# Four additions of a gate/up pair in one adding DMA, and a fourth seven-product block in the seven pairs that have it

## The chip, the cores and the metric

The kernel runs on one core of one Trainium2 chip. The metric is the device time of one execution in microseconds (us), the median of several runs.

## The reference

One decoder layer in float32 for 256 tokens, model width 2048. Two mixers (a retention branch and a sliding-window attention with sinks) work on one input projection of 2048 to 12,800 columns, are merged by two sigmoid gates, go through an output projection, and a first layer norm follows. Then comes the part that this change touches most, the feed-forward sublayer with inner width 5632, and a second layer norm:

```python
h = layer_norm(DEEPNORM_ALPHA * h + merged @ w_out[l], ln1_g[l], ln1_b[l])
ffn = (jax.nn.silu(h @ w_gate[l]) * (h @ w_up[l])) @ w_down[l]
h = layer_norm(DEEPNORM_ALPHA * h + ffn, ln2_g[l], ln2_b[l])
```

## The kernel before, in words

**Products.** Every float32 operand is split into a rounded high part and the remainder (ACT casts `wh`, DVE subtracts to get `wl`), and one product is three matmuls: high by high, high by low, low by high (L324 to L326). A matmul has 128 rows and 512 columns.

**Pairs.** Large weight matrices are worked on in pairs of 512-column blocks. For a gate/up pair `f` (class `PairChunk`, L247) the two columns are the gate's and the up's; the two rows are the two halves of the tokens. The depth of 2048 is cut into eight k pairs, each one weight load of 1 MB. An ordinary k pair ("s") is 2 x 2 x 2 = 8 products; a seven-product one ("S") computes the same from 7 products of sums (the Winograd form, L248): its step "R" has three products and its step "T" four. For S, DVE forms sums of the weights (`tsum`, L290 to L292), ACT and DVE split them (`th`, `tl`), and only three of the four original blocks are split. The sums of the left operand are made once (`hsums`, L966). The order of the k pairs is `pair_seq(n)` (L771): S and s in turn for the n seven-product ones, then the rest ordinary. `NQ` is n for gate/up pairs and `NS` for the three parts of the down projection.

A pair accumulates in eight PSUM banks, which is all of them: P1, P5, P6, P7 hold shared products, and C11, C12, C21, C22 what belongs to one result. After the last T step `mids` (L728) copies P1 (ACT) and adds the others to four tiles s1, vx, w, x5 (DVE). After the last step `done_gu` (L994) adds C11 to C22 to them and computes silu(gate) x up. Then four transposes for each half of the tokens bring it into the form that the down projection wants (`u_bg`, L922), and `psums` (L962) makes its sums.

**Parts.** The eleven pairs of the inner width (f = 0 is done by ordinary chunks) are done in parts 0 to 3, 4 to 7, 8 to 10. After each part the down projection adds its share to the residual: two down pairs after the first two parts, one and two ordinary chunks after the last.

**Order.** `Stream` (L339) issues loads, splits and matmuls step by step: loads run `LOOK_B` = 3 blocks ahead, splits as far as there are slots (three for `wh`/`wl`, one for `th`/`tl`). After each step background jobs advance by `PC` = 2 half-steps. The framework then orders each engine's queue by these priorities and adds the waits, unless an instruction is pinned in program order. Weight loads are issued on SP's queue; ACT's queue has two small loads at the start; POOL issues none.

**Start.** The first chunk loads x and its weights together in blocks of `XS` k tiles (L440). While the first one is on its way, PE runs warm-up matmuls (L434 to L438).

Of the kernel before, what the change touches and what calls it, by code (L numbers as in the profile page):

```python
# [14 lines left out]
RIGHT = "right"  # L15
# [12 lines left out]
NWARM = 3  # L28
TD = 14
CP = 1  # L30
NQ = 3
NX = 2
PG = 4
NGEN = 3
# [65 lines left out]
def layer_kernel(ctx, tc, a, out):  # L100
# [233 lines left out]
                self.done(self)  # L334

    LOOK_B = 3
    XB = 4

    class Stream:  # L339
        def __init__(self):  # L340
# [13 lines left out]
        def ahead(self):  # L354
            while True:
                cb = self.casts[min(self.ci, len(self.casts) - 1)][2]
                while self.bi < min(len(self.blocks), cb + LOOK_B):
                    ch, b = self.blocks[self.bi]
                    ch.dma(b)
                    self.bi += 1  # L360
                if self.ci >= len(self.casts):
                    return
                ch, i, _ = self.casts[self.ci]
                nm, cap = ch.slot(i)
                if self.live.get(nm, 0) >= cap:
                    return
                if self.ci in self.precast:
                    self.precast.pop(self.ci)()
                ch.cast(i)
                self.ci += 1  # L370
                self.live[nm] = self.live.get(nm, 0) + 1
# [16 lines left out]
    jobs = {}  # L388

    NC0 = P + NFR  # L390
    cst = const.tile([P, LINE * -(-NC0 // LINE)], F32, name="cst")
    ident = cst[:, 0:P]
    freq = cst[:, P:NC0]
    halfpi = const.tile([P, LINE], F32, name="halfpi")[:, 0:1]
    nc.gpsimd.memset(halfpi, math.pi / 2)

# [22 lines left out]
    dmask = msk[:, 0:RH * 384].rearrange("p (h c) -> p h c", h=RH)  # L419
    bmask = msk[:, RH * 384:]  # L420
    sinks = xa.tile([P, LINE], F32, name="sinks")[:, 0:NH]
    cosr = xa.tile([P, 2, NFL], F32, name="cosr")[:, :, 0:NFR]
    sinr = xa.tile([P, 2, NFL], F32, name="sinr")[:, :, 0:NFR]
    sinn = xa.tile([P, 2, NFL], F32, name="sinn")[:, :, 0:NFR]
# [9 lines left out]
    for i in range(NWARM):  # L434
        wp = bank("tr", [P, C])
        nc.tensor.matmul(wp, lhsT=warm[:, 0:P], rhs=warm[:, P:P + C], start=True, stop=True)
    wp = bank("tr", [P, C])
    nc.tensor.matmul(wp[:, 0:SEQ], lhsT=warm[:, 0:P], rhs=warm[:, P:P + SEQ], start=True, stop=True)  # L438

    XS = [1, 1, 2, 2, 2, 2, 2, 2, 2]  # L440
    xraw = {}

    def x_dma(b):
        k = sum(XS[:b])
        r = ini.tile([P, max(XS), SEQ + C], F32, name="xraw", bufs=XB)
        nc.sync.dma_start(out=r[:, 0:XS[b]], in_=a["xw"][:, k:k + XS[b]])
        xraw[b] = r
        if b == 2:
            nc.scalar.dma_start(out=cst[:, 0:NC0], in_=a["consts"][:, 0:NC0])
            xraw["pos"] = xa.tile([P, LINE], I32, name="posi")[:, 0:2]  # L450
            nc.scalar.dma_start(out=xraw["pos"], in_=a["pos"])

# [115 lines left out]
    def attention(g, t, q):  # L568
# [10 lines left out]
        W = nk * P  # L579
        per = C // W  # L580
        sm = ap_.tile([P, 8, W], F32, name="sm")
        mx = small.tile([P, 8], F32, name="mx8")
        sums = small.tile([P, 8], F32, name="sums")
        mk = bmask[:, P:2 * P] if t == 0 else bmask
        for j in range(4 // per):
            sps = [bank("mx", [P, per, W]) for _ in range(2)]
# [4 lines left out]
            for h, u, i in hs:  # L591
                nc.vector.tensor_tensor_reduce(out=sm[:, h], in0=sps[u][:, i], in1=mk, scale=HD ** -0.5,
                                               scalar=sinks[:, g * 8 + h:g * 8 + h + 1],
                                               op0=ALU.add, op1=ALU.max, accum_out=mx[:, h:h + 1])
        es = small.tile([P, 8], F32, name="es")
        nc.vector.tensor_sub(out=es, in0=sinks[:, g * 8:g * 8 + 8], in1=mx)
        nm = small.tile([P, 8], F32, name="nm")
        nc.vector.tensor_scalar(out=nm, in0=mx, scalar1=-1.0, scalar2=None, op0=ALU.mult)
        nc.scalar.activation(out=es, in_=es, func=AF.Exp)
        for h in range(8):  # L600
# [126 lines left out]

    def mids(ch):  # L728
        tp, acc = sc["tp"], ch.acc
        s1 = tp.tile([P, C], F32, name="s1")  # L730
        vx = tp.tile([P, C], F32, name="vx")
        w = tp.tile([P, C], F32, name="w")
        x5 = tp.tile([P, C], F32, name="x5")
        nc.scalar.copy(out=s1, in_=acc["P1"])
        nc.vector.tensor_add(out=vx, in0=s1, in1=acc["P6"])
        nc.vector.tensor_add(out=w, in0=vx, in1=acc["P5"])
        nc.vector.tensor_add(out=vx, in0=vx, in1=acc["P7"])
        nc.vector.tensor_add(out=x5, in0=vx, in1=acc["P5"])
        ev["t"] = (s1, vx, w, x5)

    def done_va(ch, j):
        acc = ch.acc
# [158 lines left out]
    sgf = {}  # L901
    ujobs = []
    parts = ((0, 4), (4, 8), (8, 11))
    NS = (3, 3, 2)
    f0_of = {f: f0 for f0, f1 in parts for f in range(f0, f1)}
    ND = {f: n for (f0, f1), n in zip(parts, NS) for f in range(f0, f1)}

    def done_g(ch, t, c):
        if t == 0:
            sgf[c] = sc["fp"].tile([P, 2, C], F32, name="sg2", bufs=1)  # L910
        nc.scalar.activation(out=sgf[c][:, t], in_=ch.acc[t], func=AF.Silu)

    def done_u(ch, t, c):
# [45 lines left out]
    def lhs_s(kp, i):  # L959
        return sc["sh"][:, i, kp], sc["sl"][:, i, kp]  # L960

    def psums(ph, pl, k0, n):  # L962
        yield
        yield from hsums(ph, pl, sc["psh"], sc["psl"], n, k0)

    def hsums(hh, hl, sh, sl_, n, k0=0):  # L966
        for kp in range(n):
            h2 = sc["tp"].tile([P, 2, 2, P], F32, name="s1")
            sm = sc["tp"].tile([P, 4, P], F32, name="vx")
            ks = slice(2 * kp, 2 * kp + 2)  # L970
            nc.vector.tensor_add(out=h2.rearrange("p k t c -> p k (t c)"), in0=hh[:, ks].bitcast(F32), in1=hl[:, ks].bitcast(F32))
            nc.vector.tensor_add(out=sm[:, 0], in0=h2[:, 0, 1], in1=h2[:, 1, 1])
            nc.vector.tensor_sub(out=sm[:, 1], in0=sm[:, 0], in1=h2[:, 0, 0])
            nc.vector.tensor_sub(out=sm[:, 2], in0=h2[:, 0, 1], in1=h2[:, 0, 0])
            nc.vector.tensor_sub(out=sm[:, 3], in0=h2[:, 1, 0], in1=sm[:, 1])
            split_evict(sh[:, :, k0 + kp], sl_[:, :, k0 + kp], sm)
            yield
# [4 lines left out]

    def flush():
        if "u" in ev:
            f, args = ev.pop("u")
            queue_p(f, [Job(u_bg(*arg)) for arg in args])

    def queue_p(f, js):
        kp = 2 * (f - f0_of[f])
        n = min(2, ND[f] - kp)  # L990
        if n > 0:
            jobs["ps", f] = Job(psums(*pTs[f], kp, n), js)

    def done_gu(ch, f):  # L994
        acc = ch.acc
        s1, vx, w, x5 = ev["t"]
        sg = sc["fp"].tile([P, 2, C], F32, name="sg2", bufs=1)
        pTs[f] = (sc["pp"].tile([P, 4, SEQ], F32R, name="ph"), sc["pp"].tile([P, 4, SEQ], F32R, name="pl"))
        nc.vector.tensor_add(out=sg[:, 0], in0=s1, in1=acc["C11"])
        nc.scalar.activation(out=sg[:, 0], in_=sg[:, 0], func=AF.Silu)  # L1000
        nc.vector.tensor_add(out=w, in0=w, in1=acc["C12"])
        nc.vector.tensor_add(out=sg[:, 1], in0=vx, in1=acc["C21"])
        nc.scalar.activation(out=sg[:, 1], in_=sg[:, 1], func=AF.Silu)
        nc.vector.tensor_mul(out=sg[:, 0], in0=sg[:, 0], in1=w)
        nc.vector.tensor_add(out=x5, in0=x5, in1=acc["C22"])
        nc.vector.tensor_mul(out=sg[:, 1], in0=sg[:, 1], in1=x5)
        ev["u"] = f, [(sg, t, *pTs[f]) for t in range(2)]
        if f + 1 in (4, 8, 11):
            flush()

    seq = pair_seq(NQ)
    for part, (f0, f1) in enumerate(parts):
        for f in range(f0, f1):
            if f == 0:
                stream.add(Chunk([a["w_gu0"][0, b] for b in range(KT // KB)], KT, lhs_h, lambda ch, t: done_g(ch, t, 0),
                                 order=stagger_first(4), wide=True))
                mark_d = len(stream.steps)
                stream.add(Chunk([a["w_gu0"][1, b] for b in range(KT // KB)], KT, lhs_h, lambda ch, t: done_u(ch, t, 0)))
                mark_u = len(stream.steps)
            else:  # L1020
                stream.add(PairChunk([a["w_gu"][f - 1, kp] for kp in range(KT // 2)], seq, lhs_h, lhs_s, mid_gu,
                                     lambda ch, f=f: done_gu(ch, f)))
        if part == 2:
            mark_e = len(stream.steps)
# [63 lines left out]
    sc["hres"] = hp.tile([P, 2, DM], F32, name="hres")  # L1088
    sc["hh"] = hp.tile([P, KT, SEQ], F32R, name="hh")
    sc["hl"] = hp.tile([P, KT, SEQ], F32R, name="hl")  # L1090
    sc["sh"] = hp.tile([P, 4, NQ, P], F32R, name="sh")
    sc["sl"] = hp.tile([P, 4, NQ, P], F32R, name="sl")
    sc["stats"] = hp.tile([P, 2, 4, 8], F32, name="stats1")[:, :, :, 0:6]
    nc.sync.dma_start(out=sc["hres"], in_=a["x"].rearrange("(t p) d -> p t d", p=P))
    gains = {}
    for nm in ("ln1_g", "ln1_b"):
# [7 lines left out]
    sc["pp"] = ppc.enter_context(tc.tile_pool(name="pp", bufs=4, side=RIGHT))  # L1104
    sc["tp"] = ppc.enter_context(tc.tile_pool(name="tp", bufs=1, side=RIGHT))
    sc["sp2"] = ppc.enter_context(tc.tile_pool(name="sp2", bufs=1, side=RIGHT))
    pq = ppc.enter_context(tc.tile_pool(name="pq", bufs=1, side=RIGHT))
    sc["psh"] = pq.tile([P, 4, max(NS), P], F32R, name="psh")
    sc["psl"] = pq.tile([P, 4, max(NS), P], F32R, name="psl")
    Job(hsums(sc["hh"], sc["hl"], sc["sh"], sc["sl"], NQ))  # L1110
    stream.run(mark_u, PC)
    banks(("all", 8))
    sc["stats"] = hp.tile([P, 2, 4, 8], F32, name="stats2")[:, :, :, 0:6]
    stream.run(mark_e, PC)
    for nm, tg in (("ln2_g", "hh"), ("ln2_b", "hl")):
        gains[nm] = hp.tile([P, DM], F32, name=tg)
        nc.sync.dma_start(out=gains[nm], in_=bcast_cols(a[nm], 0, DM))
    sc["zg"] = hp.tile([P, C], F32, name="sh")
    sc["dg"] = hp.tile([P, 2, P], F32, name="sl")
    stream.run(len(stream.steps), PC)  # L1120
    drain()

# [79 lines left out]
```

## Time and profile before

| | |
|---|---|
| median of 3 runs | 1432.5 us (1432.46 to 1432.58) |
| the profiled execution | 1432.52 us, its span 1430.7 us |
| granted TensorE clock, mean | 0.999 |
| weight loads of gate/up | 88 of 1 MB, median 4.9 us to landing |

The rows of the trace stand in a section of their own below. "Waits" give which engine and line waited for what, the sum in us, how often, and the longest. The chain is the work that ended last, followed back. A window's row gives its start and end, its length, the busy time (and number of instructions) of PE, PEld, DVE, ACT and POOL in it, the granted clock, the DMA engines' busy share and GB/s.

### The profile page before, as it was taken

What the parts mean: (1) busy time and instruction counts of PE and PEld (TensorE: products, weight loads), DVE (VectorE), ACT (ScalarE), POOL (GpSimd) and SP (SyncE); (2) the same over time, 40 slices, a digit from 0 to 9 for tenths busy, and PEclk for the clock granted to TensorE, in tenths of its full rate; (3) what the DMA queues carried; (4) which work ended last, traced back from release to release, by engine and by line L of the source; (5) the groups of instructions that cost most, each with busy time, mean ns of one, the idle gap of its engine ahead of it and who ended that gap; (6) DMA issues with size and microseconds to landing.
All of it is one profiled execution on the core that took longest, in us unless ns stands there. A gap on an engine that the chain in (4) does not pass through costs nothing.

```text
span 1430.7 us, 16141 instructions
## 1 busy us (share of the span) xinstructions
PE 1423.1 (99%) x6494; PEld 1165.0 (81%) x6494; DVE 1135.0 (79%) x1271; ACT 699.3 (49%) x664; POOL 0.9 (0%) x6
## 2 busy tenths in 40 slices
PE   9999999999999999999999999999999999999998
PEld 6878888878888878788888888888888888888886
DVE  6764555487878879776589989888999988898986
ACT  5465444344445445444345555445555455455542
POOL 0000000000000000000000000000000000000000
PEclk9999999999999999999999999999999999999999
DMA  8643433446554655567454555555555555555662
GB/s 327 222 158 118 143 115 122 150 174 210 198 209 166 210 188 206 206 244 272 160 177 177 208 184 211 193 209 193 196 195 206 206 206 181 197 211 200 213 234 88
DMA packets 40235, 274.75 MB, mean 192 GB/s; under 512 B 4704, under 2 KB 4832, under 8 KB 8160
## 3 DMA queue, kind: packets, MB, share of 16 engines
q1 hardware_dynamic: 39440, 272.79, 53.4%
q8 instruction: 51, 0.84, 0.2%
q10 hardware_dynamic: 720, 0.92, 0.2%
q14 instruction: 24, 0.20, 0.0%
HBM read 271.60 MB, written 2.10 MB: 191 GB/s over the span
## 4 chain that ended last, share of the span: by engine, by line
PE 98%; DVE 1%; DMA 0%; ACT 0%; SPq 0%; issue 0%
PE bank L324 21%; PE bank L326 21%; PE bank L325 21%; PE acc L235 9%; PE acc L233 9%; PE acc L234 9%; PE tr L540 2%; PE mx L589 2%; PE mx L618 1%; PE bank L540 1%; PE bank L235 1%; PE bank L234 1%; PE bank L233 1%; DMA xraw<-in_xw 0%; PE bank L685 0%; PE mx L656 0%
## 5 line engine op out<-in xcount | busy, mean ns | idle before, releaser
L304 ACT CAST wh<-raw 128x2048 fp32r<-128x2048 f32 (+1 forms) x174 | 307.7, 1769 | 295.1 <-PE bank L326 223.8
L305 DVE TENSOR_TENSOR wl<-raw,wh 128x2048 fp32r<-128x2048 f32 (+1 forms) x174 | 366.4, 2108 | 62.0 <-ACT wh L304 61.6
L218 DVE TENSOR_TENSOR wl<-raw,wh 128x2048 fp32r<-128x2048 f32 x70 | 160.1, 2288 | 79.6 <-ACT wh L217 79.3
L217 ACT CAST wh<-raw 128x2048 fp32r<-128x2048 f32 x70 | 133.5, 1909 | 175.0 <-PE acc L235 110.8
L324 PE MATMUL bank<-wh,hh 128*128 128x512 f32 x460 | 179.6, 390 | 0.0
L326 PE MATMUL bank<-wh,hl 128*128 128x512 f32 x460 | 179.1, 389 | 0.0
L325 PE MATMUL bank<-wl,hh 128*128 128x512 f32 x460 | 179.0, 389 | 0.0
L305 DVE TENSOR_TENSOR tl<-tsum,th 128x2048 fp32r<-128x2048 f32 x58 | 132.6, 2287 | 34.2 <-ACT th L304 34.0
L304 ACT CAST th<-tsum 128x2048 fp32r<-128x2048 f32 x58 | 111.0, 1914 | 95.1 <-DVE tsum L292 78.0
L324 PE MATMUL bank<-wh,xh 128*128 128x512 f32 x364 | 144.5, 397 | 0.0
L326 PE MATMUL bank<-wh,xl 128*128 128x512 f32 x364 | 141.8, 389 | 0.0
L325 PE MATMUL bank<-wl,xh 128*128 128x512 f32 x364 | 141.7, 389 | 0.0
L233 PE MATMUL acc<-wh,xh 128*128 128x512 f32 x352 | 140.9, 401 | 0.4 <-ACT wh L217 0.3
L235 PE MATMUL acc<-wh,xl 128*128 128x512 f32 x352 | 138.7, 394 | 0.0
L234 PE MATMUL acc<-wl,xh 128*128 128x512 f32 x352 | 138.0, 392 | 0.7 <-DVE wl L218 0.7
L326 PEld LDWEIGHTS bank<-wh,hl 128*128 128x128 f32 x460 | 86.3, 188 | 18.0
L325 PEld LDWEIGHTS bank<-wl,hh 128*128 128x128 f32 x460 | 86.4, 188 | 17.8
L324 PEld LDWEIGHTS bank<-wh,hh 128*128 128x128 f32 x460 | 86.4, 188 | 17.7
L324 PE MATMUL bank<-wh,ph 128*128 128x512 f32 x220 | 85.9, 390 | 0.0
L325 PE MATMUL bank<-wl,ph 128*128 128x512 f32 x220 | 85.6, 389 | 0.0
L326 PE MATMUL bank<-wh,pl 128*128 128x512 f32 x220 | 85.1, 389 | 0.0
L324 PEld LDWEIGHTS bank<-wh,xh 128*128 128x128 f32 x364 | 68.3, 188 | 15.8 <-issue 1.4
(287 smaller groups left out, 2315.2 us busy)
## 6 DMA issues: line engine op xcount, KB each, us to landing
raw<-in_w_gu SPq DMA_DIRECT2D x88, 1024.0 KB, 4.9
raw<-in_w_ip SPq DMA_DIRECT2D x56, 1024.0 KB, 4.9
raw<-in_w_in SPq DMA_DIRECT2D x40, 1024.0 KB, 4.9
raw<-in_w_dp SPq DMA_DIRECT2D x38, 1024.0 KB, 4.9
raw<-in_w_out SPq DMA_DIRECT2D x16, 1024.0 KB, 5.3
raw<-in_w_dl SPq DMA_DIRECT2D x6, 1024.0 KB, 4.9
xraw<-in_xw SPq DMA_DIRECT2D x7, 768.0 KB, 6.2
hres<-in_x SPq DMA_DIRECT2D x1, 2048.0 KB, 7.9
```

Source lines behind the costliest of these rows:

```text
L217: nc.scalar.copy(out=h[:, 0:m], in_=r)
L218: nc.vector.tensor_sub(out=l[:, 0:m], in0=r, in1=h[:, 0:m].bitcast(F32))
L233: nc.tensor.matmul(self.acc[t], lhsT=xh, rhs=wh[:, j], start=st, stop=False)
L234: nc.tensor.matmul(self.acc[t], lhsT=xh, rhs=wl[:, j], start=False, stop=False)
L235: nc.tensor.matmul(self.acc[t], lhsT=xl, rhs=wh[:, j], start=False, stop=sp)
L304: nc.scalar.copy(out=h_, in_=r)
L305: nc.vector.tensor_sub(out=l_, in0=r, in1=h_.bitcast(F32))
L324: nc.tensor.matmul(self.acc[p], lhsT=xh, rhs=wh[:, j], start=st, stop=False)
L325: nc.tensor.matmul(self.acc[p], lhsT=xh, rhs=wl[:, j], start=False, stop=False)
L326: nc.tensor.matmul(self.acc[p], lhsT=xl, rhs=wh[:, j], start=False, stop=sp)
L540: m = nc.tensor.transpose(ps[:, i], s, ident)
L589: nc.tensor.matmul(sps[u][:, i], lhsT=qT[u * HD:(u + 1) * HD, h // 2], rhs=kT[u * HD:(u + 1) * HD, g, 0:W], start=True, stop=True)
```

## The change

The fourth seven-product block is taken in the seven gate/up pairs that are not the last of their part (f = 1, 2, 4, 5, 6, 8, 9); in these, ACT copies the four C accumulators to one tile `cc`, and one DMA from POOL's queue adds the four `mids` tiles to it, which now are one tile `q4`. Silu and the product follow as a background job (`swish`), Silu pinned in program order. The last pairs of the parts (f = 3, 7, 10) keep three seven-product blocks and the additions on DVE. The down pair of the third part gets a third seven-product block. Sums of left operands use the `tsum` buffer and are spread over steps. At the start the x blocks are smaller and fetched further ahead, the constants come in two DMAs, and one half-width warm-up matmul is left out. Several small tiles move to other pools.

```diff
-NQ = 3
+NQ = 4
-    XB = 4
+    XB = 6
...
-                while self.bi < min(len(self.blocks), cb + LOOK_B):
+                while self.bi < min(len(self.blocks), cb + (LOOK_B if cb >= len(XS) - LOOK_B else XB - 1)):
...
-    cst = const.tile([P, LINE * -(-NC0 // LINE)], F32, name="cst")
+    cst = const.tile([P, P], F32, name="cst")
-    freq = cst[:, P:NC0]
+    freq = xa.tile([P, 3 * LINE], F32, name="freq")[:, 0:NFR]
+    sma = xsc.enter_context(tc.tile_pool(name="sma", bufs=4))
...
-    wp = bank("tr", [P, C])
-    nc.tensor.matmul(wp[:, 0:SEQ], lhsT=warm[:, 0:P], rhs=warm[:, P:P + SEQ], start=True, stop=True)
-
-    XS = [1, 1, 2, 2, 2, 2, 2, 2, 2]
+
+    XS = [1, 1, 1, 1, 2, 2, 2, 2, 2, 2]
...
-            nc.scalar.dma_start(out=cst[:, 0:NC0], in_=a["consts"][:, 0:NC0])
+            nc.scalar.dma_start(out=cst, in_=a["consts"][:, 0:P])
+            nc.scalar.dma_start(out=freq, in_=a["consts"][:, P:NC0])
...
     def mids(ch):
-        s1 = tp.tile([P, C], F32, name="s1")
-        vx = tp.tile([P, C], F32, name="vx")
-        w = tp.tile([P, C], F32, name="w")
-        x5 = tp.tile([P, C], F32, name="x5")
+        q = tp.tile([P, 4, C], F32, name="q4")
+        s1, vx, w, x5 = [q[:, i] for i in range(4)]
...
+        ev["q"] = q
...
-    NS = (3, 3, 2)
+    NS = (3, 3, 3)
...
-    def psums(ph, pl, k0, n):
-        yield
-        yield from hsums(ph, pl, sc["psh"], sc["psl"], n, k0)
+    def psums(ph, pl, k0, n, gap):
+        for _ in hsums(ph, pl, sc["psh"], sc["psl"], n, k0):
+            for _ in range(gap):
+                yield
...
-            h2 = sc["tp"].tile([P, 2, 2, P], F32, name="s1")
-            sm = sc["tp"].tile([P, 4, P], F32, name="vx")
+            ts = sc["tp"].tile([P, 4, C], F32, name="tsum")
+            h2 = ts[:, 0].rearrange("p (k t c) -> p k t c", k=2, t=2)
+            sm = ts[:, 1].rearrange("p (k c) -> p k c", k=4)
...
-            f, args = ev.pop("u")
-            queue_p(f, [Job(u_bg(*arg)) for arg in args])
+            f, args, deps = ev.pop("u")
+            queue_p(f, [Job(u_bg(*arg), deps) for arg in args])
...
-            jobs["ps", f] = Job(psums(*pTs[f], kp, n), js)
+            jobs["ps", f] = Job(psums(*pTs[f], kp, n, 14 if f < 8 else 6), js)
...
     def done_gu(ch, f):
         acc = ch.acc
         s1, vx, w, x5 = ev["t"]
-        sg = sc["fp"].tile([P, 2, C], F32, name="sg2", bufs=1)
+        cc = sc["fp"].tile([P, 4, C], F32, name="cc", bufs=1)
...
+        us = [(cc, t, *pTs[f]) for t in range(2)]
+        if f + 1 not in (4, 8, 11):
+            for i, nm in enumerate(("C11", "C21", "C12", "C22")):
+                nc.scalar.copy(out=cc[:, i], in_=acc[nm])
+            nc.gpsimd.dma_start(out=cc, in_=ev["q"], accum_op=ALU.add)
+            ev["u"] = f, us, [Job(swish(cc))]
+            return
...
+        drain()
+        ev["u"] = f, us, []
+        flush()
+
+    def swish(cc):
+        for _ in range(12):
+            yield
+        tc.keep_in_program_order(nc.scalar.activation(out=cc[:, 0:2], in_=cc[:, 0:2], func=AF.Silu))
+        yield
+        yield
+        nc.vector.tensor_mul(out=cc[:, 0:2], in0=cc[:, 0:2], in1=cc[:, 2:4])
+        yield
...
-                stream.add(PairChunk([a["w_gu"][f - 1, kp] for kp in range(KT // 2)], seq, lhs_h, lhs_s, mid_gu,
+                stream.add(PairChunk([a["w_gu"][f - 1, kp] for kp in range(KT // 2)], pair_seq(NQ - 1) if f + 1 in (4, 8, 11) else seq, lhs_h, lhs_s, mid_gu,
...
+    hq = ppc.enter_context(tc.tile_pool(name="hq", bufs=1, side=RIGHT))
+    sc["sh"] = hq.tile([P, 4, NQ, P], F32R, name="sh")
+    sc["sl"] = hq.tile([P, 4, NQ, P], F32R, name="sl")
```

## Rows read from the trace of the kernel before

**Rows 1.** The page's first part: busy us (share of the span) xinstructions of each engine.

```profile
PE 1423.1 (99%) x6494; PEld 1165.0 (81%) x6494; DVE 1135.0 (79%) x1271; ACT 699.3 (49%) x664; POOL 0.9 (0%) x6
```

**Rows 2.** Waits of PE's weight loads, 738 to 1400 us: total us, times, longest.

```profile
PEld bank L324 <- ACT th L304: 1.2, 4, 0.4
PEld bank L325 <- DVE tl L305: 0.7, 4, 0.2
PEld bank L540 <- DVE sg L1006: 0.6, 3, 0.2
PEld bank L324 <- DVE pl L402: 0.4, 1, 0.4
```

**Rows 3.** The chain of waits, whole span: start us, us, what.

```profile
837.96 0.87 PE bank L540 x8
...
946.80 1.13 PE bank L324 x5
```

**Rows 4.** Windows of pairs f = 1, 2, 4, 5, 6, 9, 10, and the last down pair.

```profile
763.00:806.30 43.30, 43.30 (x196) 35.62 (x195) 41.09 (x43) 22.15 (x16) 0.00 (x0) 1.00 0.55 194
806.30:848.50 42.20, 42.20 (x192) 35.04 (x191) 37.67 (x33) 22.01 (x16) 0.00 (x0) 1.00 0.56 199
979.50:1017.30 37.80, 37.80 (x167) 30.80 (x166) 33.51 (x26) 17.27 (x11) 0.00 (x0) 1.00 0.54 195
1017.30:1059.50 42.20, 42.20 (x192) 35.04 (x191) 38.19 (x35) 21.96 (x16) 0.00 (x0) 1.00 0.55 199
1059.50:1101.90 42.40, 42.40 (x193) 35.17 (x192) 41.23 (x46) 22.99 (x18) 0.00 (x0) 1.00 0.56 199
1270.40:1312.50 42.10, 42.10 (x191) 34.92 (x190) 38.11 (x34) 21.96 (x16) 0.00 (x0) 1.00 0.55 200
1312.50:1354.90 42.40, 42.40 (x193) 35.20 (x192) 41.20 (x45) 22.99 (x18) 0.00 (x0) 1.00 0.57 198
1354.90:1389.00 34.10, 34.10 (x156) 28.16 (x155) 27.64 (x29) 16.17 (x13) 0.00 (x0) 1.00 0.68 254
```

**Rows 5.** Timeline of PE at the start: start us, us, operation [idle before <-releaser].

```profile
9.80 0.39 PE L235 MATMUL acc<-wh,xl 128*128 128x512 f32 x1
...
11.56 0.50 PE L234 MATMUL acc<-wl,xh 128*128 128x512 f32 x1 [0.53 <-DVE wl L218]
11.90 0.39 PE L235 MATMUL acc<-wh,xl 128*128 128x512 f32 x1
```

**Rows 6.** Groups by line and shape: busy us, mean ns of one, idle before.

```profile
L305 DVE TENSOR_TENSOR tl<-tsum,th 128x2048 fp32r<-128x2048 f32 x58 | 132.6, 2287 | 34.2 <-ACT th L304 34.0
L304 ACT CAST th<-tsum 128x2048 fp32r<-128x2048 f32 x58 | 111.0, 1914 | 95.1 <-DVE tsum L292 78.0 <-PE bank L326 10.9 <-issue 5.5
L305 DVE TENSOR_TENSOR wl<-raw,wh 128x1536 fp32r<-128x1536 f32 x58 | 101.6, 1752 | 7.9 <-ACT wh L304 7.9
L290 DVE TENSOR_TENSOR tsum<-raw 128x1024 f32<-128x1024 f32 x58 | 70.7, 1220 | 5.3 <-DMA raw<-in_w_gu 3.2 <-DMA raw<-in_w_ip 1.6
L291 DVE TENSOR_TENSOR tsum<-raw,tsum 128x512 f32<-128x512 f32 x58 | 39.8, 686 | 0.8
L734 ACT COPY s<-bank 128x512 f32<-128x512 f32 x22 | 12.7, 577 | 0.0
L972 DVE TENSOR_TENSOR vx<-s 128x128 f32<-128x128 f32 x13 | 3.7, 285 | 0.1
```

**Rows 7.** DMA issues: queue, count, KB each, median us from issue to landing.

```profile
raw<-in_w_gu SPq DMA_DIRECT2D x88, 1024.0 KB, 4.9
...
ln_b<-in_ln_b SPq DMA_DIRECT2D x1, 1024.0 KB, 9.2
```

**Rows 8.** Waits over the whole span, one of DVE's: total us, times, longest.

```profile
DVE tsum L290 <- DMA raw<-in_w_gu: 3.2, 2, 2.6
```

**Rows 9.** Timeline of DVE, pair f = 1: the first and the last of the mids.

```profile
790.47 0.68 DVE L735 TENSOR_TENSOR vx<-s,bank 128x512 f32<-128x512 f32 x1
...
796.20 0.68 DVE L738 TENSOR_TENSOR x<-vx,bank 128x512 f32<-128x512 f32 x1
```

More of the change, by code (lines that the diff above doesn't have):

```diff
@@ L581, in attention @@
         sm = ap_.tile([P, 8, W], F32, name="sm")
-        mx = small.tile([P, 8], F32, name="mx8")
-        sums = small.tile([P, 8], F32, name="sums")
+        mx = sma.tile([P, 8], F32, name="mx8")
+        sums = sma.tile([P, 8], F32, name="sums")
         mk = bmask[:, P:2 * P] if t == 0 else bmask
@@ L594, in attention @@
                                                op0=ALU.add, op1=ALU.max, accum_out=mx[:, h:h + 1])
-        es = small.tile([P, 8], F32, name="es")
+        es = sma.tile([P, 8], F32, name="es")
         nc.vector.tensor_sub(out=es, in0=sinks[:, g * 8:g * 8 + 8], in1=mx)
-        nm = small.tile([P, 8], F32, name="nm")
+        nm = sma.tile([P, 8], F32, name="nm")
         nc.vector.tensor_scalar(out=nm, in0=mx, scalar1=-1.0, scalar2=None, op0=ALU.mult)
@@ L909, in done_g @@
         if t == 0:
-            sgf[c] = sc["fp"].tile([P, 2, C], F32, name="sg2", bufs=1)
+            sgf[c] = sc["fp"].tile([P, 4, C], F32, name="cc", bufs=1)
         nc.scalar.activation(out=sgf[c][:, t], in_=ch.acc[t], func=AF.Silu)
@@ L996, in done_gu @@
         s1, vx, w, x5 = ev["t"]
-        sg = sc["fp"].tile([P, 2, C], F32, name="sg2", bufs=1)
+        cc = sc["fp"].tile([P, 4, C], F32, name="cc", bufs=1)
         pTs[f] = (sc["pp"].tile([P, 4, SEQ], F32R, name="ph"), sc["pp"].tile([P, 4, SEQ], F32R, name="pl"))
-        nc.vector.tensor_add(out=sg[:, 0], in0=s1, in1=acc["C11"])
-        nc.scalar.activation(out=sg[:, 0], in_=sg[:, 0], func=AF.Silu)
+        us = [(cc, t, *pTs[f]) for t in range(2)]
[5 more added lines that the diff above has]
+            return
+        nc.vector.tensor_add(out=cc[:, 0], in0=s1, in1=acc["C11"])
+        nc.scalar.activation(out=cc[:, 0], in_=cc[:, 0], func=AF.Silu)
         nc.vector.tensor_add(out=w, in0=w, in1=acc["C12"])
-        nc.vector.tensor_add(out=sg[:, 1], in0=vx, in1=acc["C21"])
-        nc.scalar.activation(out=sg[:, 1], in_=sg[:, 1], func=AF.Silu)
-        nc.vector.tensor_mul(out=sg[:, 0], in0=sg[:, 0], in1=w)
+        nc.vector.tensor_add(out=cc[:, 1], in0=vx, in1=acc["C21"])
+        nc.scalar.activation(out=cc[:, 1], in_=cc[:, 1], func=AF.Silu)
+        nc.vector.tensor_mul(out=cc[:, 0], in0=cc[:, 0], in1=w)
         nc.vector.tensor_add(out=x5, in0=x5, in1=acc["C22"])
[L1006 to L1009, printed above, removed]
+        nc.vector.tensor_mul(out=cc[:, 1], in0=cc[:, 1], in1=x5)
+        drain()
[9 more added lines that the diff above has]
+        yield
     seq = pair_seq(NQ)
@@ L1090, in layer_kernel @@
     sc["hl"] = hp.tile([P, KT, SEQ], F32R, name="hl")
-    sc["sh"] = hp.tile([P, 4, NQ, P], F32R, name="sh")
-    sc["sl"] = hp.tile([P, 4, NQ, P], F32R, name="sl")
-    sc["stats"] = hp.tile([P, 2, 4, 8], F32, name="stats1")[:, :, :, 0:6]
+    sc["stats"] = hp.tile([P, 2, 4, 8], F32, name="stats")[:, :, :, 0:6]
     nc.sync.dma_start(out=sc["hres"], in_=a["x"].rearrange("(t p) d -> p t d", p=P))
@@ L1112, in layer_kernel @@
     banks(("all", 8))
-    sc["stats"] = hp.tile([P, 2, 4, 8], F32, name="stats2")[:, :, :, 0:6]
+    sc["stats"] = hp.tile([P, 2, 4, 8], F32, name="stats")[:, :, :, 0:6]
     stream.run(mark_e, PC)
@@ L1117, in layer_kernel @@
         nc.sync.dma_start(out=gains[nm], in_=bcast_cols(a[nm], 0, DM))
-    sc["zg"] = hp.tile([P, C], F32, name="sh")
-    sc["dg"] = hp.tile([P, 2, P], F32, name="sl")
+    sc["zg"] = hq.tile([P, C], F32, name="sh")
+    sc["dg"] = hq.tile([P, 2, P], F32, name="sl")
     stream.run(len(stream.steps), PC)
```

## The prediction

> **What bounds the kernel now.** I read the page's first part, then the waits of TensorE in the feed-forward stage, then the chain of waits, then DVE's idle time window by window. The page says that PE is busy for 99% of the span, with DVE at 79%, ACT at 49% and POOL idle [rows 1]. A busy PE may still be a stalled one, so the second view asks what the weight loads waited for between 738 and 1400 us: four kinds of wait, 2.9 us together out of 662 us [rows 2]. PE is therefore the bound almost everywhere, and the price of a matmul is its pitch in the chain: five in 1.13 us, so 0.226 us each, while eight transposes take 0.87 us [rows 3]. A pair of NQ=3 has 183 matmuls and eight transposes, 41.4 + 0.87 = 42.2 us, which is how far apart the pairs' ends lie in the windows of [rows 4]. The same windows show who is next: DVE. In the pairs its idle time is window length less DVE busy time, 4.5 us in the lightest full pair and 1.2 us in the heaviest [rows 4], and PE lost nothing even there. So matmuls taken away count in full, until DVE has no time left for the casts they need.
>
> **The change part by part.** The profiled execution took 1432.52 us (span 1430.7), the same as the median of 1432.5, so I start from 1432.5.
>
> *Matmuls.* A seven-product block has 7 x 3 matmuls instead of 8 x 3. Seven pairs (f = 1, 2, 4, 5, 6, 8, 9) get a fourth such block, and the down chunk of the third part a third one: 8 x 3 = 24 matmuls, 24 x 0.226 = **-5.4 us**, all on the path [rows 3]. The number and size of the weight loads on SP's queue stay as they are.
>
> *The start.* The x blocks become 1,1,1,1,2,... k tiles and are fetched further ahead. Between 9.80 us, when the last matmul before this gap starts, and 11.90 us the trace has four steps where four pitches are 0.9 us: the double block is cast late, and its low half holds PE [rows 5]. So at most 1.2 us comes back, and at worst nothing. I take **-0.8 us**, because the block behind keeps its size and so its casts; the value is nearer to the row than to zero. The removed half-width warm-up matmul stood before the first data, while PE had to wait anyway. The extra DMA issue on ACT's queue (the constants in two pieces) stands before the first x data too. Both count nothing; if that cover were gone, the issue would cost some 0.4 us.
>
> *DVE's work.* A fourth seven-product block adds one 128x1024 and two 128x512 subtractions and a 128x2048 one for the sums, and narrows the other from 2048 to 1536 columns: 1.22 + 2 x 0.69 + 2.29 - (2.29 - 1.75) = 4.3 us [rows 6]. A DMA pair loses four additions of this 128x512 shape, 0.69 us each, and its two products of 0.69 us become one that I price as the other 128x1024 operation, 1.22 us [rows 6]: -2.9 us. Net +1.5 us, in a pair that is 0.7 us shorter. Because the additions fall into the window of the next pair, I book by window. The pairs without such an end before them (f = 1, 4, 8) lose 4.3 + 0.7 = 5.0 us of idle time, pairs 2, 5, 6, 9 lose 2.2, and pairs 3, 7, 10 win 2.9. Out of 2.2 us in the first window of [rows 4], f = 1 comes to -2.8; f = 2 from 4.5 to 2.3; f = 4 from 4.3 to -0.7; f = 5 from 4.0 to 1.8; f = 6 from 1.2 to -1.0; f = 8 as f = 4; f = 9 from 4.0 to 1.8; f = 10 from 1.2 to 1.6, since the new third sum for the down chunk (two 128x512 operations, four of 128x128 at 0.28 us, 2.5 us) goes there; the down chunk from 6.5 to 1.5 [rows 4, 6]. The spread-out sums (the gap of 14 or 6) move such work within this account. So four windows are short by 2.8 + 0.7 + 1.0 + 0.7 = 5.2 us. The bounds: if casts already done ahead cover it, PE loses 0; if each of these windows also wants the 1.2 us of idle time that the heaviest window kept, 10.0 us. For how far ahead the casts are, the trace has three slots of split weights: after a slot is free, a cast of 1.9 us and its subtraction of 2.29 us [rows 6] must be done within two steps, 24 + 9 matmuls or 7.5 us [rows 3], so some 3 us can be lent once to a run of short windows. I take half of the shortage, **+2.6 us**, nearer the lower end, since windows at 1.2 us of idle time ran without loss.
>
> *The adding DMA.* It moves 1 MB within SBUF; no row shows one. The nearest rows are plain loads of 1 MB, 4.9 us from issue to landing alone and 9.2 us behind another [rows 7]. Its Silu is pinned 12 half-steps after the pair's end, that is two blocks of each kind or 90 matmuls, 20 us [rows 3]; four copies of 0.58 us [rows 6] and 9.2 us make 11.5. So ACT should not wait, and behind it in ACT's queue no cast is held. POOL has nothing else to do [rows 1] and nothing is queued behind. I cost it at nothing; the cover is the remaining 8.5 us. The Trainium skill says in "Collectives: The Full Stack", Stop 4 (SDMA + CCE) and the bandwidth part, that an add in the DMA path costs its second source read, about half the rate; by that I estimate twice the plain load, 9.8 us, still inside the cover, and no run here shows it yet.
>
> *ACT and the rest.* ACT gains four copies (2.3 us), one cast of 1.9 us less 0.4, and loses little, out of 20 us idle in each pair [rows 4]: nothing, as an amount. Pool moves and separate small tiles carry no work. Hand the sums the shared tsum buffer and a cast may queue behind them; that is in DVE's upper bound.
>
> Sum: 1432.5 - 5.4 - 0.8 + 2.6 = **1428.9 us**.
>
> **The rivals.** Differences within 0.2% (2.9 us) are about what a measurement of this kernel cannot tell from no change.
>
> *Everything hidden.* DVE's shortage is lent by casts done ahead. For it: the waits of PE were 2.9 us in 662 with DVE at 97% in two windows [rows 2, 4]. Against it: the windows turn negative by my account. Time: 1432.5 - 6.2 = 1426.3 us.
>
> *The adding DMA delays weight loads.* Some loads already land just as they are wanted: the tsum operation waited for one twice, 2.6 us the longest [rows 8]. A load that shares the engines with the adding DMA can land 4.9 us later; less the 3 us of lead above, 1.8 us is lost where that hits. If it hits two of seven, 3.6 us: 1432.5 us, the change does nothing. If it hits all, 12.6 us. Against: DMA is busy for 0.55 of these windows only [rows 4].
>
> *Slower: the PSUM banks at a pair's end.* A pair holds all eight banks. With a fourth block the five "mids" operations come one ordinary step before the end instead of three. In the trace they take from 790.47 to 796.88 us, 6.4 us [rows 9], since casts go in between. Behind them stand the four copies out of PSUM, 2.3 us [rows 6], which in pairs that follow a DMA pair must wait until the old tile is transposed, 0.87 us [rows 3]. That is 9.6 us, where PE reaches for its fourth new bank after 24 + 9 matmuls, 7.5 us. Seven times 2.1 us is 14.7, and PE's waiting gives DVE its time back, so the 2.6 goes: 1426.3 + 14.7 = 1441.0 us. It decides for slower from 9.2 us in all, 1.3 us a pair, on. Against: four banks are freed one by one, and copies of the first two accumulators can start six matmuls early.
>
> *Descriptors held back.* If the adding DMA started only when DVE pauses, in the windows with 1.2 us of pause [rows 4] it could come 20 us late and hold ACT, and the casts behind it, for about 10 us; less the 3 us of lead, two such windows cost 14 us: 1443 us. The rows show only tensor_tensor work on DVE in these pairs. The Trainium skill tells of this in "SBUF — State Buffer", the box on DVE blocking a DMA that POOL issues, and says there too, under who interferes with whom, that tensor_tensor has no such mode; no run here shows either.
>
> **How the numbers follow.** Forecast (part of the gain given back to DVE) 0.40; everything hidden 0.20; loads delayed, no change 0.20; banks 0.15; descriptors 0.05. The forecast's own spread is 1426 to 1431, about a sixth of it inside 0.2%: faster 0.20 + 0.33 = 0.53; same 0.07 + 0.20 = 0.27; slower, with the two last cases, 0.20. The range runs from the matmuls and the whole start gap without any stall, 1432.5 - 5.4 - 1.2 = 1425.9, to 1437, which takes in the loads' case and about a third of the banks' case, at 1.5 us a pair; it leaves out 0.15 at the top.
>
> **What would show it.** In the changed profile: PE has 24 + 1 program matmuls fewer (the warm-up one), the start's gap is shorter, and the pitch stays 0.226 us. DVE's idle time in the windows of f = 1, 4 and 6 is close to nothing. Waits of PE's weight loads grow to 2 to 5 us, on th, tl, wh or wl. The Silu of the DMA pairs shows no long wait for the DMA. If these waits stay at 3 us, everything was hidden. If instead PE waits for DVE's or ACT's bank readers at the pair ends, or DVE for raw loads, a rival holds. I am wrong by mechanism if the pairs get longer although DVE has idle time and all banks are free.

## The result, and the profile after

The change makes the kernel slower. Its median is 1466.1 us (1463.0 to 1467.0, four runs) against 1432.5 us before (1432.46 to 1432.66); the ratio is 1.0231, with a 95% interval from 1.0213 to 1.0248. The profiled execution took 1463.0 us (span 1461.2). The other three ran at a granted clock of 0.995 to 0.996 where it had 0.999, and took some 2 to 4 us more. I compare traces with the profiled execution: its span is 30.5 us longer than before.

The shares of the chain before (part 4 of the page), and behind them the page of the changed kernel, parts 1, 4 and 6 (engines, shares of the chain, the new DMA with its size and median to landing):

```profile
PE 98%; DVE 1%; DMA 0%; ACT 0%; SPq 0%; issue 0%
```

```profile
PE 1431.5 (98%) x6468; PEld 1158.3 (79%) x6468; DVE 1158.1 (79%) x1282; ACT 724.7 (50%) x697; POOL 7.0 (0%) x13
...
PE 85%; DVE 6%; DMA 3%; ACT 3%; issue 2%; SPq 0%; ACTq 0%
...
cc<-q POOLq DMA_DIRECT2D x7, 1024.0 KB, 7.7
```

DVE is as busy, as a share, as before [rows 1], and PE has 26 instructions fewer. Nevertheless only 85% of the chain runs on PE, where it was 98%. What PE's weight loads waited for between 738 and 1400 us (total us, times, longest) shows where:

```profile
PEld bank L324 <- ACT th L304: 22.7, 31, 2.7
PEld bank L325 <- DVE wl L305: 7.3, 8, 1.6
PEld bank L325 <- DVE tl L305: 3.7, 10, 2.0
PEld bank L540 <- DVE cc L1012: 3.1, 2, 2.6
PEld bank L324 <- DVE q L735: 2.8, 3, 1.0
```

All waits together were 2.9 us before [rows 2]. Now PE waits for split weights, above all for the cast `th` of a weight sum. Windows from pair to pair (f = 1, 2, 4, 5, 7, 9, last down pair; columns as in [rows 4]) give the place:

```profile
761.90:806.20 44.30, 42.62 (x189) 34.10 (x188) 39.96 (x37) 24.34 (x19) 0.00 (x0) 1.00 0.56 191
806.20:856.40 50.20, 43.97 (x190) 33.84 (x188) 42.85 (x40) 23.97 (x18) 1.00 (x1) 1.00 0.63 208
...
987.80:1029.30 41.50, 41.45 (x181) 33.55 (x180) 35.87 (x29) 20.88 (x15) 0.00 (x0) 1.00 0.52 190
1029.30:1074.00 44.70, 42.90 (x189) 34.15 (x187) 40.19 (x33) 24.27 (x18) 0.86 (x1) 1.00 0.69 227
...
1117.70:1165.80 48.10, 45.10 (x192) 36.14 (x193) 42.75 (x40) 26.17 (x24) 0.86 (x1) 0.96 0.60 201
...
1292.40:1338.50 46.10, 42.95 (x190) 34.19 (x188) 40.20 (x33) 24.26 (x18) 0.86 (x1) 1.00 0.67 221
...
1382.10:1418.20 36.10, 32.67 (x143) 25.64 (x143) 33.67 (x33) 18.91 (x15) 0.00 (x0) 1.00 0.71 264
```

A pair of four S blocks has 180 matmuls and eight transposes: 180 x 0.226 + 0.87 = 41.6 us. So f = 2 loses 50.2 - 41.6 = 8.6 us, f = 9 4.5, f = 5 3.1; f = 7, with three blocks but behind three pairs of four, loses 48.1 - 42.2 = 5.9, of which its granted clock of 0.96 can account for 1.9 (0.04 x 48.1). But f = 4, which has four blocks and comes behind a down pair that ends in ordinary steps (no transposes at its start, so 40.7 us), loses only 0.8 us. Thus a fourth block isn't dear in itself. And DVE is idle for 50.2 - 42.85 = 7.4 us in the worst window, more than the 4.5 us of the same pair before [rows 4]: it has time and waits.

For what, the DMA queue tells. SP's waits between 738 and 1400 us, before:

```profile
SPq L282 <- DVE wl L305: 453.8, 92, 10.9
SPq L282 <- DVE tsum L292: 74.5, 22, 8.5
```

and after:

```profile
SPq L282 <- DVE wl L305: 311.2, 64, 10.8
SPq L282 <- DVE tsum L292: 202.1, 49, 13.3
SPq L282 <- DMA raw<-in_w_gu: 60.9, 25, 4.9
```

SP waits here for a free raw buffer. A buffer of an S block is free only after L292, the last subtraction of the weight sum, and L292 needs the one `tsum` buffer. Before, that was the releaser of 22 loads, now of 49. The chain at the beginning of f = 2 (start us, us, what) shows what follows:

```profile
808.40 1.76 DVE wl L305
810.16 0.60 DVE psl L401
810.76 0.07 DVE q L736
810.83 0.44 issue
811.28 1.22 DVE tsum L290
812.49 2.20 DVE wl L305
814.70 0.61 DVE tsum L291
815.31 0.02 issue
815.33 0.70 DVE tsum L292
816.03 0.02 issue
816.05 10.07 DMA raw<-in_w_gu
...
826.20 1.02 ACT wh L304
827.22 0.79 issue
828.01 1.91 ACT th L304
829.92 0.04 issue
829.96 1.19 PE bank L324 x4
```

The sums of the down operand sit in `tsum` until psl at 810.16; only then L290 starts, L292 ends at 816.03, a load is issued at 816.05, takes 10.07 us (the adding DMA is on its way from 811.9 to 820.0, and another load since 814.7), and ACT, DVE and PE follow it at once. Nothing of a lead is left in this chain.

### The profile page after: what moved, and what is told of

It reads as the page before. It is cut to its first block, busy times and chain, and to the rows that moved or that the text cites. A ratio compares the mean times of both kernels' runs of the same rounds, so it can differ in the third digit from the quotient of the medians.

```text
span 1461.2 us, 16170 instructions
## 1 busy us (share of the span) xinstructions
PE 1431.5 (98%) x6468; PEld 1158.3 (79%) x6468; DVE 1158.1 (79%) x1282; ACT 724.7 (50%) x697; POOL 7.0 (0%) x13
## 4 chain that ended last, share of the span: by engine, by line
PE 85%; DVE 6%; DMA 3%; ACT 3%; issue 2%; SPq 0%; ACTq 0%
PE bank L324 17%; PE bank L325 17%; PE bank L326 17%; PE acc L233 8%; PE acc L235 8%; PE acc L234 8%; DMA raw<-in_w_gu 3%; DVE wl L305 2%; ACT wh L304 2%; PE tr L540 2%; PE mx L589 1%; PE mx L618 1%; ACT th L304 1%; DVE tl L305 1%; PE bank L235 1%
## 5 line engine op out<-in xcount | busy, mean ns | idle before, releaser
L305 DVE TENSOR_TENSOR wl<-raw,wh 128x2048 fp32r<-128x2048 f32 (+1 forms) x174 | 362.5, 2085 | 84.5 <-ACT wh L304 83.9
L305 DVE TENSOR_TENSOR tl<-tsum,th 128x2048 fp32r<-128x2048 f32 x66 | 151.0, 2288 | 24.2 <-ACT th L304 23.6
L325 PE MATMUL bank<-wl,hh 128*128 128x512 f32 x418 | 163.9, 392 | 2.8 <-DVE wl L305 2.8
L324 PE MATMUL bank<-wh,hh 128*128 128x512 f32 x418 | 163.6, 394 | 2.9 <-DVE q L735 2.1
L326 PE MATMUL bank<-wh,hl 128*128 128x512 f32 x418 | 161.8, 391 | 0.0
L304 ACT CAST th<-tsum 128x2048 fp32r<-128x2048 f32 x66 | 125.9, 1908 | 59.4 <-DVE tsum L292 56.0
L324 PEld LDWEIGHTS bank<-wh,hh 128*128 128x128 f32 x418 | 78.6, 188 | 21.6 <-DVE q L735 2.8
L325 PEld LDWEIGHTS bank<-wl,hh 128*128 128x128 f32 x418 | 78.8, 188 | 20.6 <-DVE wl L305 4.5
L326 PEld LDWEIGHTS bank<-wh,hl 128*128 128x128 f32 x418 | 78.8, 188 | 16.5
L290 DVE TENSOR_TENSOR tsum<-raw 128x1024 f32<-128x1024 f32 x66 | 80.4, 1218 | 2.3 <-DMA raw<-in_w_ip 1.9
```

The costliest lines, as they stand in the source:

```text
L290: nc.vector.tensor_sub(out=x[:, 0:2], in0=r[:, 0:1].broadcast_to([P, 2, C]), in1=r[:, 1:4:2])
L304: nc.scalar.copy(out=h_, in_=r)
L305: nc.vector.tensor_sub(out=l_, in0=r, in1=h_.bitcast(F32))
L324: nc.tensor.matmul(self.acc[p], lhsT=xh, rhs=wh[:, j], start=st, stop=False)
L325: nc.tensor.matmul(self.acc[p], lhsT=xh, rhs=wl[:, j], start=False, stop=False)
L326: nc.tensor.matmul(self.acc[p], lhsT=xl, rhs=wh[:, j], start=False, stop=sp)
```

## The experiments

Theories: (A) the adding DMA delays weight loads; (B) with four S blocks no two ordinary steps follow one another, so nothing rebuilds the lead (the time by which loads and splits run ahead of PE); (C) the left operand's sums hold `tsum`; (D) the one `th`/`tl` slot is too little for a block every 33 matmuls; (E) the one `tsum` buffer holds raw buffers, so loads go out late. D and E were formed after the first four experiments. All but the last two kernels ran once, and I compare them with the 1463.0 us of the profiled execution; the kernel before, run beside them, took 1432.4 to 1432.7 us. The changed kernel's own four runs lie 4 us apart, so a difference of that size between two single runs is not shown to come from the edit.

**Three blocks, all else as changed.**

```diff
-... pair_seq(NQ - 1) if f + 1 in (4, 8, 11) else seq, ...
+... pair_seq(NQ - 1), ...
```

> All gate/up pairs keep three seven-product blocks; the adding DMA, the sums in the tsum buffer and the rest of the change stay. Theory A (the adding DMA delays weight loads that were about to be used): most of the 39 us lost in the feed-forward stage stay, 1455 to 1462 us. Theory B (the fourth block leaves no ordinary steps behind it, so every delay of a cast is passed on): nearly all of it goes, 1430 to 1436 us. Theory C (sums of the left operands hold the tsum buffer): part of it goes, since the ordinary steps at a pair's end take them in; 1433 to 1445 us.

1433.3 us (before: 1432.4). The fourth block, 21 matmuls fewer, makes the difference of 30 us. SP waits in the same window:

```profile
SPq L282 <- DVE wl L305: 427.9, 88, 10.7
SPq L282 <- DVE tsum L292: 89.4, 25, 8.5
```

That is nearly the picture of before, and PE's waits for `th` are 4.6 us instead of 22.7. B holds as to the place. Where ordinary steps follow, the adding DMA, the sums in `tsum` and the rest cost little: 2.9 us against the kernel with the start and the third block alone, 1430.4 us (the last experiment).

**Four blocks, additions on DVE in all pairs.**

```diff
-        if f + 1 not in (4, 8, 11):
+        if False:
...
-        drain()
         ev["u"] = f, us, []
-        flush()
+        if f + 1 in (4, 8, 11):
+            drain()
+            flush()
```

> Four seven-product blocks in the seven pairs, and the four additions, both Silu and both products done as before on DVE and ACT; no adding DMA. Theory A: without the DMA the loads land in time and the loss goes, 1430 to 1440 us. Theory B: DVE has 1.5 us more work per pair than with the DMA and the lockstep stays: 1463 us or more. Theory C: the sums still hold the tsum buffer: 1455 to 1470 us.

1471.5 us, 8.5 us more than with the DMA. So A is not the main cause. Some of the 8.5 is TensorE's clock: 10-us windows of this kernel, two of them with PE idle for 3.3 and 4.3 us and one right behind (columns as in [rows 4]):

```profile
1128.00:1138.00 10.00, 6.75 (x22) 4.75 (x21) 10.00 (x11) 2.17 (x2) 0.00 (x0) 0.83 0.31 107
...
1388.00:1398.00 10.00, 5.71 (x24) 3.82 (x22) 10.00 (x13) 6.49 (x7) 0.00 (x0) 0.91 0.98 411
1398.00:1408.00 10.00, 9.66 (x35) 7.89 (x36) 7.96 (x10) 3.87 (x3) 0.00 (x0) 0.75 0.26 80
```

Full clock is 2.4 GHz, the lower level 1.2. The windows below 1.00 miss 0.85 in sum, up to 8.5 us; in the changed kernel two windows miss 0.17, 1.7 us. Without that the two kernels differ by some 2 us, within what single runs can tell: the DMA seems to save DVE about as much as it costs.

**An eighth of the adding DMA** (the additions of the other seven eighths of the columns are left out).

```diff
-nc.gpsimd.dma_start(out=cc, in_=ev["q"], accum_op=ALU.add)
+nc.gpsimd.dma_start(out=cc[:, :, 0:64], in_=ev["q"][:, :, 0:64], accum_op=ALU.add)
```

> The adding DMA moves 64 of each 512 columns, an eighth of the bytes; the additions of the other columns are left out. All else is as in the changed kernel. Theory A: it no longer delays loads: below 1440 us. Theories B and C: the order and the waits of all engines stay, so 1458 to 1467 us.

1457.8 us: the transfer's size is worth 5 us of the 30, or 8 to 9 with the clock taken out as above (its windows miss 0.51). A counts, as a minor part. The load that took 10.07 us in the changed kernel is issued at the same moment here, 816.1 us, and takes 6.8.

**The sums of left operands in q4 instead of tsum.**

```diff
-ts = sc["tp"].tile([P, 4, C], F32, name="tsum")
+ts = sc["tp"].tile([P, 4, C], F32, name="q4" if "pp" in sc else "tsum")
```

> The sums of the left operands in the feed-forward stage use the buffer of the mids instead of the tsum buffer. Theory C: the weight sums of the next seven-product block are no longer held up, waits of th for tsum and of loads for L292 shrink: 1435 to 1450 us. Theories A and B: little changes, 1460 to 1467 us.

1455.3 us: 8 us, or 9 with the clock taken out (its windows miss 0.34), a part again. It moves the loss as well: q4 is held by the adding DMA, for which DVE now waits with the sums (four times between 738 and 1400 us, 9.3 us in all, 4.3 the longest), and the weight sums behind them in its queue wait too.

**No sums of the down operand** (they are left out; the down pairs read `sh`, `sl` in their place, as many matmuls).

```diff
-jobs["ps", f] = Job(psums(*pTs[f], kp, n, 14 if f < 8 else 6), js)
+jobs["ps", f] = Job(iter(()), js)
...
-sc["psh"] = pq.tile([P, 4, max(NS), P], F32R, name="psh")
-sc["psl"] = pq.tile([P, 4, max(NS), P], F32R, name="psl")
+sc["psh"], sc["psl"] = sc["sh"], sc["sl"]
```

> The sums of the down pairs' left operands are left out (the down pairs use those of the gate/up pairs, whose values are wrong for them); this frees 12 KB of SBUF in each partition, and is the base for the next two. Theory C as part of the cause: what went when the sums were moved out of the tsum buffer goes here too, and DVE has 9 x 2.5 us less to do: 1445 to 1455 us. If the sums were all of it: below 1435 us.

1447.5 us (before: 1432.7). The sums are worth 15 us (14 with the clock taken out; this kernel's windows miss nothing), which leaves another 15 with the sums gone. That is not the hold on `tsum` alone (C): their work on DVE and ACT goes with them, and the experiment before, which kept the work and moved only the hold, brought 8 to 9. The kernel has 12 KB a partition less in use, and the experiments without the down sums build on it.

**No additions of mids in the four-block pairs** (left out; the DMA adds another tile).

```diff
-seq, lhs_h, lhs_s, mid_gu,
+seq, lhs_h, lhs_s, mid_gu if f + 1 in (4, 8, 11) else mid_gu4,
...
+    def mid_gu4(ch):
+        s1 = sc["tp"].tile([P, 4, C], F32, name="q4")[:, 0]
+        nc.scalar.copy(out=s1, in_=ch.acc["P1"])
...
+        ev["q"] = sc["hres"][:, 0].rearrange("p (i c) -> p i c", i=4)
...
```

> In the seven pairs with four blocks the four mids additions on DVE are left out; the adding DMA reads the residual tile instead. Theory D (between the last T step and the next pair's first T step there are now 33 matmuls, 7.5 us, instead of 81, and in them th and tl, which have one slot each, the mids and the copies must all be done): 4 x 0.6 us of DVE leave just that stretch, so at least half of the loss goes, 1440 to 1450 us. Theory E (the raw buffer of a seven-product block is held until L292, which waits for the one tsum buffer, so weight loads are issued late): little changes, 1457 to 1465 us.

1453.1 us: 10 us, less than D wanted (13 and more) and more than E did (6 at most). DVE's work at the pair's end is a part of the loss, not the main one; I take it to be one of the things that come between L290 and L292, which no run isolates.

**Two tsum buffers, without the down sums.**

```diff
-x = sc["tp"].tile([P, 4, C], F32, name="tsum")
+x = sc["tp"].tile([P, 4, C], F32, name="tsum", bufs=2 if "pp" in sc else 1)
...
```

> As e7, with two tsum buffers in the feed-forward stage. Theory E: weight sums run ahead, raw buffers come free earlier, loads land in time: 10 us or more below e7, and SP's waits on L292 shrink. Theory D: the window for th and tl stays: within 4 us of e7.

1432.4 us: 15.1 us less than with one buffer, and the time of the kernel before. SP waits with one buffer and no down sums:

```profile
SPq L282 <- DVE wl L305: 358.0, 67, 10.5
SPq L282 <- DVE tsum L292: 139.6, 48, 8.5
```

and with two:

```profile
SPq L282 <- DVE wl L305: 536.5, 110, 9.3
SPq L282 <- DVE tsum L292: 26.7, 5, 7.0
```

L292 is the releaser of 5 loads instead of 48. No wait for `th` is left among PE's, with the whole adding DMA and four blocks in place. That also bears on A: six loads beside the adding DMAs took 9.4 to 9.9 us here, where the changed kernel has one over 9, and the loss is gone all the same.

**Two th buffers, without the down sums.**

```diff
-return ("sp2", 1) if self.steps[i][0] == "T" else ("spl", NSPL)
+return ("sp2", 2 if "pp" in sc else 1) if self.steps[i][0] == "T" else ("spl", NSPL)
...
-h = sc["sp2"].tile([P, KS, C], F32R, name="th")
+h = sc["sp2"].tile([P, KS, C], F32R, name="th", bufs=2 if "pp" in sc else 1)
```

> As e7, with two th buffers (and one tl) in the feed-forward stage, so that the high part of the weight sums can be cast before the T step before is over. Theory D: PE's waits on th (23 us in the changed kernel) go, and 8 us or more against e7; waits on tl may take their place in part. Theory E: the cast comes earlier, but the load behind it does not: within 4 us of e7.

1447.0 us, 0.5 us less (some 2 with the clock taken out: its windows miss 0.17, those of the kernel without the down sums nothing). D falls, as far as the slot of `th` goes; `tl` kept its one slot.

**A fourth raw buffer, one tsum, without the down sums.** This takes the two jobs of `tsum` apart: holding a raw buffer, and making the sum itself late.

```diff
-r = rawp.tile([P, KB, C], F32, name="raw")
+r = raw_tile()
...
+    def raw_tile():
+        if "pp" in sc:
+            nraw[0] += 1
+            if nraw[0] % 4 == 1:
+                return sc["tp"].tile([P, KB, C], F32, name="raw4")
+        return rawp.tile([P, KB, C], F32, name="raw")
...
-... cb + (LOOK_B if cb ...
+... cb + (LOOK_B + ("pp" in sc) if cb ...
```

> As the kernel without the down sums (its psh and psl left out, so that SBUF has room), with one tsum buffer as there, but a fourth buffer for raw weights and loads one block further ahead in the feed-forward stage. If the loss comes from raw buffers that are freed late, by the last subtraction of a sum that waits for tsum, the fourth buffer covers it: a wait of SP on that subtraction costs nothing any more, DVE, ACT and PE stop waiting for raw loads, and the time falls from 1447.5 to 1431 to 1436 us, as with two tsum buffers (1432.4). If what matters in tsum is that the sum itself, and so its cast and its subtraction, are ready late, an earlier load does not help and the time stays at 1444 to 1448 us. In between, both count, in that proportion.

1441.1 us, 6.4 of the 15.1 us. SP still waits for L292, 47 times, but now a block ahead, and no wait for a raw load is left among ACT's or DVE's. PE's waits in this kernel:

```profile
PEld bank L324 <- ACT th L304: 10.8, 25, 1.2
PEld bank L324 <- DVE q L744: 4.1, 4, 1.0
PEld bank L325 <- DVE wl L305: 4.0, 4, 1.0
```

With one tsum and three raw buffers the first row reads 16.8 us. So E is right but not the whole: about four tenths of what the second `tsum` buffer brings is the loads. The rest I put down to the sum itself, which can't begin before the sum before it has been split; the waits for `th` that are left speak for it, and no run takes it alone.

**The start alone, and the third block of the down pair.** The first has only the edits at the start on the kernel before (the smaller x blocks, fetched further ahead, and the warm-up matmul left out, not the constants in two DMAs); the second adds a line.

```diff
-    NS = (3, 3, 2)
+    NS = (3, 3, 3)
```

> The kernel before with the change's edits at the start of the program alone, three S blocks as before and no adding DMA. The account by which the whole loss comes from the weight loads beside the fourth block: the first gate/up pair starts 2.6 us earlier (761.9 us after, 764.5 us before) and nothing else moves, so 1429.5 to 1430.5 us. The account by which the start changes bring a loss later, by shifting the loads against the blocks: 1432 us or more.

> As the kernel with the start changes alone, with three S blocks in the last down pair too, where the kernel before has fewer. By the loads account a pair with three S blocks and ordinary steps behind them loses nothing: in the kernel with three blocks and the adding DMA that pair took 0.7 us less than before, so 1428.7 to 1430 us, some 3 us under the kernel before. If the third block there costs as the fourth does in a gate/up pair (4 us and more each), 1433 us or more.

1430.5 and 1430.4 us against 1432.55 (11 runs each and 21): ratio 0.9985 for both, interval 0.9976 to 0.9994. The start is a real gain of 2.1 us; the third block brings nothing: its down pair became 0.1 us shorter for three matmuls, 0.7 us. These two are the fastest that keep the whole computation, and the only ones clearly under the kernel before.

## Why the prediction was wrong

**Matmuls.** The term of -5.4 us was right in what it counted, and waits took back more than all of it. The pitch stayed (0.23 us a piece in the chain), but a matmul taken away shortens the time only where the weights of the next one are ready.

**The start.** I took -0.8 us. In the kernel with the start alone, PE's timeline (as in [rows 5]) has

```profile
12.37 0.39 PE L235 MATMUL acc<-wh,xl 128*128 128x512 f32 x1
12.60 0.61 PE L233 MATMUL acc<-wh,xh 128*128 128x512 f32 x2
13.55 0.50 PE L234 MATMUL acc<-wl,xh 128*128 128x512 f32 x1 [0.34 <-DVE wl L218]
13.89 0.39 PE L235 MATMUL acc<-wh,xl 128*128 128x512 f32 x1
```

Four steps in 1.52 us lose 0.6 us, where they lost 1.2 [rows 5], and the first product starts at 6.32 us instead of 6.66: 0.9 us in all, the size that I took. The other 1.2 us of the 2.1 come later, in the mixers' stage, whose first pair starts at 320.4 us instead of 322.8; I didn't trace them further.

**The step that failed** stands in the paragraph on matmuls: "The number and size of the weight loads on SP's queue stay as they are", and so the sum has no term for them. Their number stayed, but not the moment at which each goes out, which depends on what frees its buffer. A fourth block turns one ordinary step's release, by `wl`, into one by L292, behind a single buffer that `wl`, `th`, `tl` and the new `hsums` all stand in the way of. I had the last of these in one sentence, "Hand the sums the shared tsum buffer and a cast may queue behind them; that is in DVE's upper bound", which priced as a quantity of DVE's work what is a hold on a buffer. Leaving those sums out was worth 15 us, a second buffer another 15.

**DVE as an amount of work.** I booked work against idle time and let 3 us be lent. But windows that I booked as the safest lost most: f = 2, with 2.3 us to spare by that account, lost 8.6 us while DVE's idle time grew to 7.4; f = 4, booked as short by 0.7, lost 0.8, which agrees by chance, since DVE was idle there for 41.5 - 35.9 = 5.6 us. An engine can be idle for longer because it is late. What counts is the lead, and in the kernel before two or more ordinary steps at each pair's end had rebuilt it; with three blocks and everything else changed, 1433.3 us, they still do.

**The adding DMA.** It landed in 7.1 to 9.4 us, within the 9.2 that I took (but for one). The estimate of 9.8 us in the prediction lies above all seven. The Silu behind the one in the window of f = 2 starts at 829.8 us, 9.8 us after landing; the cover said 8.5. But "I cost it at nothing" was wrong on its other side: a load beside it took 10.07 us, where the median is 4.9 and the longest before was 7.9. The rival on delayed loads had a load land 4.9 us later. Of this load's 5.2 us over the median 3.3 go with the transfer (6.8 us with an eighth of it); the rest fits the load issued 1.3 us before it. The rival's 12.6 us for seven hits (13.3 with its own 4.9 - 3) are more than the 5 to 9 measured by shrinking the transfer. As the cause of the whole it falls: without the DMA the kernel is slower still, and with two `tsum` buffers loads nearly as slow go with the time of before.

**The slower rivals.** *Banks*: PE's waits for their readers (`q`, `cc`, not those of the transposes) are some 4 us, not 14.7; the additions of mids cost 10 us, which I put down to the weight sums that they delay. *Descriptors*: no DMA landed late in the changed kernel (with three blocks one took 12.1 us), in windows with DVE 85 to 92% busy with tensor_tensor work. The Trainium skill, "SBUF — State Buffer", under who interferes with whom, says that a probe found `tensor_copy` stalling a DMA, and `tensor_tensor` not. The seven landings of at most 9.4 us agree.

**What I had named as the sign of being wrong**, longer pairs "although DVE has idle time and all banks are free", is nearly what the trace shows.

The sum, put right: 1432.5 - 5.4 (matmuls) - 2.6 (f = 1 starts at 761.9 instead of 764.5 us) = 1424.5, and PE's losses behind the start of f = 1, which grow by 38.5: from there to the end of the span it is 1461.2 - 761.9 = 699.3 us, before 1430.7 - 764.5 = 666.2, with 5.4 us less to do. That makes 1463.0 us. Nor was the term of +2.6 us for DVE's work what was lost: in each of the windows above DVE is idle for 2.4 us or more. Of these 38.5, about 15 go with the down sums, 15 with the second buffer, and 8 are left in the kernel with two buffers, half of them in f = 1 (46.1 - 41.6 = 4.5). I don't split them further by sums over experiments: the parts overlap (leaving out the mids' additions alone gave 10).

Open: a version with the down sums and two `tsum` buffers wasn't tried (the second buffer's 8 KB a partition came from the 12 that the down sums had); so it isn't shown that four blocks can ever gain. Even the kernel with two buffers and no down sums only reaches the time of before.

## What to carry to other kernels

When a change replaces a step by one that holds buffers differently, follow each load back to the instruction that frees its buffer, and that one to the buffer it needs itself; equal numbers of loads say nothing. Idle time of a feeding engine is no reserve where steps are chained through a single buffer: ask which steps rebuild the lead, and what is left when the last of them goes. A saving of 0.7 us a pair was bought with the only slack that the pair had.

## What the runs showed of the hardware

An accumulating DMA of 1 MB within SBUF took 7.1 to 9.4 us (median 7.7) beside weight loads in the changed kernel, and 8.1 to 12.1 in the one with three blocks; an eighth of it took 3.5 to 3.9. A 1 MB load of weights issued while one was on its way took 10.07 us, and in the kernel with two `tsum` buffers up to 9.9; without the adding DMA the longest took 8.0. And some of PE's stalls were followed by a stretch below the full clock, a mean of 0.66 to 0.96 over 10 us, though not all (in the changed kernel's f = 2, with PE idle for 6.2 us in sum, it stayed 1.00). The kernel with most of them lost up to 8.5 us by it.
